# Spreading the preparation of the last weight matrix over the branch stage of a hybrid attention and retention step

## Chip, cores and metric

The kernel runs on one NeuronCore of a Trainium2 chip. The metric is the device time of one execution in microseconds (us); lower is better.

## What is computed

One layer of a streaming encoder on 2048 prompt frames and 64 sample frames of width 1024, all in fp32. The part that matters here is the end of the layer:

```python
def layer_output(x, oa, ob, za, zb, ga, gb, subln_g, lam_init, w_oa, w_ob, w_out):
    oa = (rmsnorm(oa, subln_g) * (1.0 - lam_init)).reshape(B, T, W_A) * jax.nn.silu(za)
    ob = rmsnorm(ob).reshape(B, T, W_B) * jax.nn.silu(zb)
    m = ga * (oa @ w_oa) + gb * (ob @ w_ob)      # the branch stage
    return x + m @ w_out                         # the last stage
```

`oa` and `ob` are the outputs of differential attention and of retention (512 columns each), `za`, `zb`, `ga`, `gb` come from a combined input projection, and `w_out` is 1024x1024.

## The kernel before

Each fp32 product is three matmuls on operands split in a high part (a cast to fp32r) and a low part (the fp32 value less its high part): high by high, high by low, low by high. A cast on ACT and a subtraction on DVE or POOL make the two parts.

The program is written by generators ("tasks") that a small loop advances by a cost model of its own. That loop fixes the order of the instructions on PE, ACT, DVE and POOL. The order of the DMAs, which all go through SyncE's queue (SP), is set afterwards by the framework's scheduler; SP then runs them strictly in that order, each waiting for what it needs. On every engine an instruction that waits holds up all that stand behind it.

Until 1576 us the projections, attention and retention run (matmul line L554 last). Then come:

- The **branch stage** (1576 to 1772 us). The 2112 frames are eight token groups of 264 columns. A group has eight tiles `ct` (128 rows of m each); a tile is 12 matmuls into PSUM bank `mm` (branch a) and 12 into bank `s` (branch b), two buffers each (L1722 to L1724). DVE multiplies each bank by its gate (L1742), which frees the bank; POOL adds the two (L1746); SP stores the sum to `mT` in DRAM. Groups and tiles are counted from 0 here, stores `mT` from 1 to 64.
- Its operands: `z` and `on` (132 KB each) are loaded, ACT takes silu of `z` (L1664), POOL multiplies (L1667), ACT casts to `ogh` (L1677), DVE subtracts to `ogl` (L1680). Four of these make the operands of one branch of one group (a "quad"). There is room for three quads: two in the tag `og`, one in the tag `ob`. A quad's casts wait until PE has finished with the quad three before it. Gates `gt` are loaded in pairs for one tile (10 buffers) and pass through ACT (L1698).
- The **preparation of w_out** (`b_prep`): w_out is used in blocks of Strassen's form. For each of four slices `c` it loads four pieces of 256 KB (`wst<-in_w_out_dram`), forms sums on DVE (L1758, four a slice) and splits seven blocks on ACT (L1815) and DVE (L1818). Slices 0 and 1 are split fully; of slices 2 and 3 the four sums t1 to t4 are held and split late (`b_late`) after tile 3 of group 7, when the buffers of w_o are free.
- The **last stage** (1772 us to the end): for each group seven products P1, P2, P6, P5, P7, P3, P4 of 12 matmuls (L1934) in banks `mm`, `s`, `at`. Their left operands are sums of quarters of m, loaded back from `mT` (`a<-mT`): s1, s2 on DVE (L1758), s3, s4 on POOL (L1756), split by L1853 and L1860. `y_prep` loads the quarters a11 and a12 of group 0; `y_load` loads all four quarters of each group for the sums. ACT copies the finished bank out as `u` (L1962), POOL adds the residual x (`oxt`), DVE finishes (L1984).

The buffers of the last stage (`u`, `oxt`, `ah`, `al`) and of w_out lie where earlier stages had theirs: the w_out blocks and `ob` over the buffers of the projections (among them `ev`, from which the last gates are stored by `gbT<-ev`), and `u`, `oxt`, `ah`, `al` over the gates of the branch stage.

Of the kernel before, what the change touches and what calls it, by code (L numbers as in the profile page):

```python
# [59 lines left out]
class Hybrid:  # L60
# [1573 lines left out]
    def out_prep(self):  # L1634
        pa = self.z3p
        self.wo = [[([[self.sb(self.zq, [128, 512], "wa", "woq", F32R) for n in "hl"],
                      [pa.tile([128, 512], F32R, tag=f"wo{n}{br}{kt}", name=f"wo{n}{br}{kt}") for n in "hl"]], {})
                    for kt in range(4)] for br in range(2)]
        for br in range(2):
            yield from self.load_wo(br, 0)  # L1640
        for g in range(8):
            gsl = slice(GW * g, GW * g + GW)
            for br, (oT, zT) in enumerate(((self.oaT, self.zaT), (self.obT, self.zbT))):
                for kt in range(4):
                    yield from self.take("oz", 2)
                    on = self.sb(pa, [128, GW], "oz", "on")
                    z = self.sb(pa, [128, GW], "oz", "z")
                    self.ld(z, zT[kt][:, gsl], 1 << 17)
                    t = self.ld(on, oT[kt][:, gsl], 1 << 17)
                    og = []  # L1650
                    self.ogs.append(og)
                    self.spawn(self.og_fin(on, z, t, og, (2 * g + br) % 3 == 2), 1)
                    yield self.pe
            if g == 0:
                self.spawn(self.gates(), 0)
                for q in range(1, 4):
                    for br in range(2):
                        yield from self.load_wo(br, q)
                yield lambda: self.b_left < 13

    def og_fin(self, on, z, t, og, third):
        nc = self.nc
# [98 lines left out]
    def b_raw(self, c, pool, tag):  # L1761
        w = self.i["w_out"][0]
        raw = {}
        for k, r, n in (("11", c, 0), ("12", c, 512), ("22", c + 4, 512), ("21", c + 4, 0)):
            yield from self.take(tag)
            raw[k] = self.sb(pool, [128, 512], tag, "wst")
            t = self.ld(raw[k], w[128 * r:128 * r + 128, n:n + 512], 1 << 18)
            self.b_left -= 1
        yield t + 600
        return raw  # L1770

    def b_prep(self):
        late = []
        for c in range(4):
            raw = yield from self.b_raw(c, self.z4, "st")
            for k in ("t1", "t2"):
                yield from self.take("st")
                raw[k] = self.sb(self.z4, [128, 512], "st", "wst")
            t1 = self.add(False, ALU.subtract, raw["t1"], raw["12"], raw["11"], self.pe)
            for k in ("11", "21", "22"):  # L1780
                t = yield from self.b_split(k, c, raw[k], self.pe)
            t3 = self.add(False, ALU.subtract, raw["12"], raw["22"], raw["12"], t)
            self.give("st", t3)
            yield t3
            t2 = self.add(False, ALU.add, raw["t2"], raw["12"], raw["11"], t3)
            self.give("st", t2)
            yield t2
            t4 = self.add(False, ALU.subtract, raw["21"], raw["21"], raw["t2"], t2)
            parts = [("t2", c, raw["t2"], t4), ("t1", c, raw["t1"], t1), ("t3", c, raw["12"], t3),
                     ("t4", c, raw["21"], t4)]  # L1790
            if c < 2:
                yield from self.b_fin(parts)
            else:
                late.append(parts)
        self.spawn(self.b_late([p for pair in zip(*late) for p in pair]), 1)
        self.spawn(self.y_prep(), 1)
# [24 lines left out]
        return t  # L1821

    def y_load(self):
        yield lambda: len(self.wt["t4"]) == 4
        for g in range(8):
            yield lambda: self.y_at >= g - 1 and len(self.mt[g]) == 8
            yield max(self.mt[g])
            raw = {}
            for k in ("a11", "a21", "a22", "a12"):
                raw[k], t = yield from self.y_raw(g, k)  # L1830
            self.yr.append((raw, t + 600))
# [223 lines left out]

    def out_stream(self):
        for g in range(8):
            og = []
            for ct in range(8):
                yield from self.m_tile(g, ct, og)  # L2060
        self.spawn(self.y_open(), 0)
        yield from self.y_group()
# [112 lines left out]
    def run(self):  # L2175
        tc, nc = self.tc, self.nc
        es = self.es = ExitStack()
        self.scratch()
        self.cp = es.enter_context(tc.tile_pool(name="cp", bufs=1))
        self.pp = es.enter_context(tc.tile_pool(name="pp", bufs=2, space=PSUM))  # L2180
        self.sp = es.enter_context(tc.tile_pool(name="small", bufs=6))
        z1 = self.z1 = ExitStack()
        z2 = self.z2 = ExitStack()
        self.ap = z1.enter_context(tc.tile_pool(name="att", bufs=ROWS, side="right"))
        self.tp_ = z1.enter_context(tc.tile_pool(name="tmp", bufs=1, side="right"))
        self.ep = z2.enter_context(tc.tile_pool(name="evac", bufs=2))
        self.wp = z2.enter_context(tc.tile_pool(name="wts", bufs=2))
        self.xp = z2.enter_context(tc.tile_pool(name="xT", bufs=1))
        nc.scalar.preload_act_table_set("natural_log_exp_and_others")
        self.marks = {}  # L2190
        self.gts, self.ya = {}, {}
        self.mt = [[] for _ in range(8)]
        self.wt = {k: [] for k in BLOCKS}
        self.b_left = 16
        for k in ("ac", "u", "xt", "ob"):
            self.res[k].free = []
        self.q_end = self.smx = None
        self.y_at, self.yr = -1, []
        self.yq = [{} for _ in range(8)]
        ET = mybir.EngineType  # L2200
        with tc.manual_schedule(engines=MANUAL(ET)):
            self.ident = self.cp.tile([128, 128], F32, tag="ident", name="ident")
            self.xraw = {(half, seg): [] for half in range(2) for seg in range(2)}
            self.xin = self.xsq = self.xfree = self.wloads = 0
            self.xacc = []
            self.xst, self.opened, self.rsb_of = None, False, None
            self.xr = [[None] * KC for _ in range(2)]
            self.rst, self.spread_ok, self.tb = [[], []], False, [None] * 9
            self.rs = self.cp.tile([128, 2, 10], F32, tag="rs", name="rs")
            self.ep_ = self.cp.tile([128, 2, 10], F32, tag="ep", name="ep")  # L2210
            self.gx = self.cp.tile([128, 8], F32, tag="gx", name="gx")
            self.ld(self.gx, self.i["norm_g"][0].rearrange("(c p) -> p c", p=128))
            self.ones_r = self.cp.tile([128, 128], F32R, tag="ones", name="ones")
            self.ones = self.ones_r.bitcast(F32)
            nc.vector.memset(self.ones, 1.0 / 128.0)
            self.epst = self.cp.tile([128, 1], F32, tag="epst", name="epst")
            nc.vector.memset(self.epst, EPS)
            self.warm(15)
            self.pe = 0.0
            self.spawn(self.consts(), 0)  # L2220
            self.spawn(self.w_stream(), 9)
            self.spawn(self.z_stream(), 4)
            self.loop()
        es.close()


def MANUAL(ET):
    return {ET.PE, ET.Activation, ET.DVE, ET.Pool}
# [65 lines left out]
```

## Time and profile before

| | us |
|---|---|
| Three runs: lowest, median, highest | 1944.82, 1947.86, 1949.27 |
| The profiled execution | 1945.97 |
| Its span in the trace | 1944.2 |
| Branch stage in the trace | 1576.1 to 1772.3 |
| Last stage in the trace | 1772.3 to 1944.2 |

The mean granted clock of TensorE is 0.999. Rows of an engine's timeline show the start, the duration, the line, the instruction and its tiles; in brackets stands how long the engine was idle before it and what ended that. The row count `x8` merges neighbours. PE's durations overlap: a 128x264 matmul lasts about 0.28 us, and one starts every 0.12 us. Rows of SPq are the issues of DMAs, not the transfers.

### The profile page before, as it was taken

The numbers are of one execution on the slowest core, as the hardware profiler recorded it, in microseconds if no ns is written. First come the engines' busy times: TensorE is split into PE (matmuls) and PEld (weight loads), VectorE is DVE, ScalarE is ACT, GpSimd is POOL, SyncE is SP. The second block draws the span as 40 slices with busy tenths as digits, with TensorE's granted clock in tenths as the row PEclk, the third lists the DMA queues.
The fourth block names the chain that finished last, engine by engine and source line by source line (L and its number), as shares of the span: only waits on it lengthen the run. The fifth ranks groups of instructions, "written<-read, shape, count | busy, mean of one in ns | idle before, by whom it ended". The sixth has DMA issues, their size and how long they took to land.

```text
span 1944.2 us, 33842 instructions
## 1 busy us (share of the span) xinstructions
PE 1927.8 (99%) x11984; PEld 1729.5 (89%) x11984; DVE 1163.8 (60%) x2798; ACT 967.3 (50%) x2072; POOL 488.8 (25%) x429
## 2 busy tenths in 40 slices
PE   9999999999999999999999999999999999999999
PEld 8779999999988899999998888888888889998887
DVE  6753777646666336648856757745764366545643
ACT  6443766544434235535765646544563455653321
POOL 4310112212121121211121112112112356543422
PEclk9999999999999999999999999999999999999999
DMA  7757554335566655664344253363233678866652
GB/s 230 242 154 196 143 147 129 107 104 155 164 193 186 163 151 164 202 187 142 112 116 131 72 146 101 95 182 118 68 98 103 187 233 265 265 191 195 191 147 66
DMA packets 372074, 303.32 MB, mean 156 GB/s; under 512 B 77440, under 2 KB 334720, under 8 KB 371904
## 3 DMA queue, kind: packets, MB, share of 16 engines
q1 hardware_dynamic: 371904, 301.16, 52.9%
q8 instruction: 94, 1.54, 0.3%
q14 instruction: 76, 0.62, 0.1%
HBM read 195.87 MB, written 100.14 MB: 152 GB/s over the span
## 4 chain that ended last, share of the span: by engine, by line
PE 89%; DVE 4%; DMA 2%; ACT 1%; issue 1%; POOL 1%; SPq 1%; DVEq 0%; ACTq 0%; POOLq 0%
PE mm L554 51%; PE mm L1934 4%; PE s L1052 3%; PE s L1053 3%; PE at L1160 3%; PE at L1934 2%; PE pv L1140 2%; PE pv L1139 2%; PE pv L1138 2%; PE mm L1722 1%; PE s L1723 1%; PE mm L1723 1%; PE mm L1724 1%; PE s L1724 1%; PE s L1934 1%
## 5 line engine op out<-in xcount | busy, mean ns | idle before, releaser
L514 POOL TENSOR_TENSOR wl<-ws,wh 128x512 fp32r<-128x512 f32 x191 | 261.4, 1379 | 897.0 <-ACT wh L504 552.7
L554 PE MATMUL mm<-xh,wh 128*128 128x512 f32 (+2 forms) x1280 | 460.7, 360 | 0.0
L554 PE MATMUL mm<-xh,wl 128*128 128x512 f32 (+2 forms) x1280 | 453.2, 354 | 0.0
L554 PE MATMUL mm<-xl,wh 128*128 128x512 f32 (+2 forms) x1280 | 451.5, 353 | 0.0
L554 PEld LDWEIGHTS mm<-xh,wl 128*128 128x128 f32 x1280 | 240.9, 188 | 32.1
L554 PEld LDWEIGHTS mm<-xh,wh 128*128 128x128 f32 x1280 | 241.2, 188 | 29.1 <-issue 0.2
L554 PEld LDWEIGHTS mm<-xl,wh 128*128 128x128 f32 x1280 | 241.5, 189 | 28.4
L554 PE MATMUL mm<-wh,xh 128*128 128x256 f32 (+1 forms) x768 | 236.8, 308 | 0.0
L554 PE MATMUL mm<-wh,xl 128*128 128x256 f32 (+1 forms) x768 | 231.3, 301 | 0.0
L554 PE MATMUL mm<-wl,xh 128*128 128x256 f32 (+1 forms) x768 | 231.3, 301 | 0.0
L1175 DVE TENSOR_TENSOR atl<-at,ath 128x512 fp32r<-128x512 f32 (+1 forms) x144 | 93.7, 659 | 136.2 <-ACT ath L1173 136.0
L504 ACT CAST wh<-ws 128x512 fp32r<-128x512 f32 x192 | 116.9, 617 | 112.3 <-PE mm L554 91.6
L1091 ACT ACTIVATE row<-row,a_mx 128x1024 f32<-128x1024 f32 (+7 forms) x160 | 153.7, 962 | 24.7 <-DVE a_mx L1071 24.6
L554 PEld LDWEIGHTS mm<-wh,xh 128*128 128x128 f32 x768 | 146.4, 191 | 7.2 <-issue 0.5
L554 PEld LDWEIGHTS mm<-wl,xh 128*128 128x128 f32 x768 | 146.5, 191 | 6.8 <-issue 0.5
L554 PEld LDWEIGHTS mm<-wh,xl 128*128 128x128 f32 x768 | 146.3, 191 | 5.6
L865 DVE TENSOR_TENSOR ev<-mm,rsb 128x512 f32<-128x512 f32 x140 | 83.0, 593 | 112.2 <-PE mm L554 110.4
L1173 ACT CAST ath<-at 128x512 fp32r<-128x512 f32 (+1 forms) x144 | 78.7, 563 | 141.9 <-PE at L1160 138.9
L1061 DVE CUSTOM_DVE_ANT_0 row<-s,dfar 128x512 f32<-128x512 f32 (+2 forms) x192 | 118.3, 630 | 46.3 <-PE s L1053 45.9
L1052 PE MATMUL s<-K,q 128*128 128x512 f32 (+3 forms) x320 | 118.3, 374 | 0.7 <-DVE a_acc L1061 0.7
L1053 PE MATMUL s<-K,q 128*128 128x512 f32 (+3 forms) x320 | 115.4, 363 | 0.0
L1110 ACT ACTIVATE row<-row,a_w 128x1024 f32<-128x1024 f32 (+4 forms) x96 | 85.1, 898 | 34.4 <-DVE a_w L1105 31.2
(342 smaller groups left out, 4188.1 us busy)
## 6 DMA issues: line engine op xcount, KB each, us to landing
ws<-in_w_in_dram SPq DMA_DIRECT2D x192, 256.0 KB, 3.1
q<-qT SPq DMA_DIRECT2D x128, 128.0 KB, 3.1
V<-vN SPq DMA_DIRECT2D x24, 512.0 KB, 5.5
K<-kT SPq DMA_DIRECT2D x48, 256.0 KB, 4.2
a<-mT SPq DMA_DIRECT2D x34, 256.0 KB, 4.2
gt<-gaT SPq DMA_DIRECT2D x64, 132.0 KB, 3.1
gt<-gbT SPq DMA_DIRECT2D x64, 132.0 KB, 3.0
mT<-gt SPq DMA_DIRECT2D x64, 132.0 KB, 3.1
```

Source lines behind the costliest of these rows:

```text
L504: self.nc.scalar.copy(h, st)
L514: self.nc.gpsimd.tensor_sub(l, st, h.bitcast(F32))
L554: nc.tensor.matmul(ps, p, q, start=c == 0 and i == 0, stop=c == KC - 1 and i == 2)
L865: nc.vector.tensor_mul(ev, ps, rsb)
L1052: nc.tensor.matmul(ps, q1s, kk, start=True, stop=False)
L1053: nc.tensor.matmul(ps, q2s, kk, start=False, stop=True)
L1061: nc.vector.tensor_tensor_reduce(out=units[k0 // 1024][:, k0 % 1024:k0 % 1024 + n], in0=ps, in1=tab, scale=-SLOPES[h], scalar=3.0e38, op0= ...
L1091: nc.scalar.activation(u, u, AF.Exp, bias=mx, scale=-1.0, accum_out=lp[:, k:k + 1])
L1110: nc.scalar.activation(u1, u1, AF.Identity, scale=w[:, 1:2])
L1173: nc.scalar.copy(ah[:, :w], at[:, :w])
L1175: nc.vector.tensor_sub(al[:, :w], at[:, :w], ah[:, :w].bitcast(F32))
L1934: nc.tensor.matmul(q[b], u, v, start=fresh and c == 0 and m == 0, stop=c == 3 and m == 2, skip_group_check=True)
```

## The change

`b_prep` now starts slice c at the beginning of token group 1, 3, 5 and 6 (`self.mg` is the group whose matmuls are being written out), where it ran through all four slices as fast as buffers allowed. `out_prep` no longer holds back the operands of group 1 until the first four pieces of w_out have been requested. `y_load` starts when three t1 blocks are split, where it waited for the fourth t4 block.

```diff
 def out_prep(self):
             if g == 0:
                 self.spawn(self.gates(), 0)
                 for q in range(1, 4):
                     for br in range(2):
                         yield from self.load_wo(br, q)
-                yield lambda: self.b_left < 13
 def b_raw(self, c, pool, tag):
             t = self.ld(raw[k], w[128 * r:128 * r + 128, n:n + 512], 1 << 18)
-            self.b_left -= 1
 def b_prep(self):
         late = []
-        for c in range(4):
+        for c, g in enumerate((1, 3, 5, 6)):
+            yield lambda: self.mg >= g
             raw = yield from self.b_raw(c, self.z4, "st")
 def y_load(self):
-        yield lambda: len(self.wt["t4"]) == 4
+        yield lambda: len(self.wt["t1"]) > 2
 def out_stream(self):
         for g in range(8):
-            og = []
+            og, self.mg = [], g
```

PE's order is the same, instruction for instruction; the other engines' orders are the same up to the start of the branch stage. Line numbers behind L1659 are one lower in the changed kernel.

**Start of the branch stage, DVE, before.** `gt<-gt,mm` and `gt<-gt,s` are the gate products of tiles 0, 1, 2; `wst` and `bl` belong to slice 0 of w_out; `ogl` is the low part of the first operand of group 1.

```order
L865 TENSOR_TENSOR ev_18280<-mm_18253,rsb_8967 128x512
L1742 SCALAR_TENSOR_TENSOR gt_17950<-gt_17950,mm_18331 128x264
L1742 SCALAR_TENSOR_TENSOR gt_17951<-gt_17951,s_18344 128x264
L1742 SCALAR_TENSOR_TENSOR gt_17954<-gt_17954,mm_18357 128x264
L1742 SCALAR_TENSOR_TENSOR gt_17955<-gt_17955,s_18373 128x264
L1758 TENSOR_TENSOR wst_18401<-wst_18305,wst_18303 128x512
L1818 TENSOR_TENSOR bl11_18290<-wst_18303,bh11_18289 128x512
L1742 SCALAR_TENSOR_TENSOR gt_17958<-gt_17958,mm_18387 128x264
L1742 SCALAR_TENSOR_TENSOR gt_17959<-gt_17959,s_18408 128x264
L1818 TENSOR_TENSOR bl21_18292<-wst_18309,bh21_18291 128x512
L1680 TENSOR_TENSOR ogl_18414<-on_18311,ogh_18413 128x264
```

The same place in the changed kernel:

```order
L865 TENSOR_TENSOR ev_18311<-mm_18269,rsb_8967 128x512
L1679 TENSOR_TENSOR ogl_18342<-on_18233,ogh_18341 128x264
L1679 TENSOR_TENSOR ogl_18346<-on_18237,ogh_18345 128x264
L1679 TENSOR_TENSOR ogl_18349<-on_18249,ogh_18348 128x264
L1679 TENSOR_TENSOR ogl_18352<-on_18253,ogh_18351 128x264
L1741 SCALAR_TENSOR_TENSOR gt_17950<-gt_17950,mm_18354 128x264
L1741 SCALAR_TENSOR_TENSOR gt_17951<-gt_17951,s_18379 128x264
L1741 SCALAR_TENSOR_TENSOR gt_17954<-gt_17954,mm_18398 128x264
L1741 SCALAR_TENSOR_TENSOR gt_17955<-gt_17955,s_18420 128x264
L1741 SCALAR_TENSOR_TENSOR gt_17958<-gt_17958,mm_18437 128x264
```

The four subtractions of group 1's first quad moved ahead of the first gate product, and the work on w_out left this place (it begins behind the gate product of tile 9).

**The same place in SP's queue, before:** the last store of the gates (`gbT<-ev`) and what follows it.

```order
L140 DMA gbT<-ev 128x2x256
L135 DMA wst<-in_w_out_dram 128x512 x4
L140 DMA mT<-gt 128x264 x2
L135 DMA gt<-gaT 128x264
L135 DMA gt<-gbT 128x264
L135 DMA on<-obT 128x264
L135 DMA z<-zbT 128x264
```

And in the changed kernel:

```order
L140 DMA gbT<-ev 128x2x256
L135 DMA wst<-in_w_out_dram 128x512 x2
L135 DMA z<-zaT 128x264
L135 DMA on<-oaT 128x264
L135 DMA z<-zaT 128x264
L135 DMA on<-oaT 128x264
L135 DMA z<-zaT 128x264
L135 DMA on<-oaT 128x264
L140 DMA mT<-gt 128x264
```

Six loads for group 2 stand ahead of the first store of a sum; five loads of group 1's branch b (`z<-zbT`, `on<-obT`), which followed the w_out pieces, now stand ahead of the `gbT` store. From the first w_out piece up to the gate load of tile 16, SP issues 71 DMAs before and 64 now; from there to the gate load of tile 24, 47 before and 44 now. Before, w_out pieces 9 to 16 stood between the stores `mT` 15 and 22; now pieces 5 to 8 stand between `mT` 12 and 15, pieces 9 to 12 between 28 and 31, and 13 to 16 between 44 and 47.

**Start of the last stage, POOL, before** (the last two additions of gates, the residual of P1, then s4 and s3):

```order
L1746 TENSOR_TENSOR gt_21107<-gt_21107,gt_21108 128x264
L1746 TENSOR_TENSOR gt_21154<-gt_21154,gt_21155 128x264
L1756 TENSOR_TENSOR u_21322<-u_21322,oxt_21299 128x512
L1756 TENSOR_TENSOR a_21341<-a_21249,a_21333 128x512
L1756 TENSOR_TENSOR a_21245<-a_21243,a_21245 128x512
```

And in the changed kernel:

```order
L1745 TENSOR_TENSOR gt_21107<-gt_21107,gt_21108 128x264
L1755 TENSOR_TENSOR a_21281<-a_21174,a_21259 128x512
L1755 TENSOR_TENSOR a_21150<-a_21144,a_21150 128x512
L1745 TENSOR_TENSOR gt_21164<-gt_21164,gt_21165 128x264
L1755 TENSOR_TENSOR u_21327<-u_21327,oxt_21329 128x512
```

s4 and s3 moved ahead of the last addition of gates. On SP, likewise, the four loads of group 1's quarters moved ahead of the last store `mT`; before:

```order
L135 DMA a<-mT 128x4x128 x3
L140 DMA mT<-gt 128x264 x4
L135 DMA oxt<-in_x_prompt_dram 128x512 x10
L135 DMA a<-mT 128x4x128 x4
L135 DMA oxt<-in_x_prompt_dram 128x512
```

now:

```order
L135 DMA a<-mT 128x4x128 x3
L140 DMA mT<-gt 128x264 x3
L135 DMA a<-mT 128x4x128 x4
L140 DMA mT<-gt 128x264
L135 DMA oxt<-in_x_prompt_dram 128x512 x12
```

The three `a<-mT` ahead of it are the rest of group 0's quarters, at the same place in both.

More of the change, by code (lines that the diff above doesn't have):

```diff
@@ L2193, in run @@
         self.wt = {k: [] for k in BLOCKS}
-        self.b_left = 16
+        self.mg = -1
         for k in ("ac", "u", "xt", "ob"):
```

## Prediction

> **What bounds the kernel now.** I read the busy times of the page first, then the stretches of the two stages that the change touches, then the timelines of PE, ACT, DVE and SP at each place where PE was idle. The page says that PE is the bound:
>
> ```profile
> span 1944.2 us, 33842 instructions
> PE 1927.8 (99%) x11984; PEld 1729.5 (89%) x11984; DVE 1163.8 (60%) x2798; ACT 967.3 (50%) x2072; POOL 488.8 (25%) x429
> ```
>
> PE's order and work don't change, so only PE's stalls, and a reduced clock behind them, can be won or lost. The stretches of the branch stage and of the last stage (length, then busy time and instructions of PE, weight loads, DVE, ACT, POOL, then granted clock, DMA share, GB/s) tell how much that is:
>
> ```profile
> 1576.10:1600.00 23.90, 23.11 (x187) 22.70 (x186) 18.62 (x29) 12.41 (x31) 15.61 (x17) 1.00 0.66 203
> 1600.00:1624.00 24.00, 23.82 (x196) 23.60 (x195) 19.23 (x34) 14.93 (x35) 16.38 (x17) 1.00 0.87 267
> 1624.00:1648.00 24.00, 22.85 (x186) 22.44 (x186) 16.68 (x33) 14.32 (x35) 14.14 (x17) 1.00 0.88 260
> 1648.00:1672.00 24.00, 21.26 (x157) 20.42 (x156) 14.44 (x31) 14.13 (x34) 14.46 (x16) 0.93 0.88 264
> 1672.00:1700.00 28.00, 28.00 (x232) 28.00 (x231) 12.92 (x30) 18.28 (x44) 14.56 (x19) 1.00 0.91 266
> 1700.00:1716.00 16.00, 15.94 (x131) 15.73 (x131) 8.53 (x19) 8.23 (x21) 8.67 (x12) 1.00 0.77 221
> 1772.30:1794.40 22.10, 20.17 (x87) 15.81 (x86) 9.69 (x14) 5.50 (x10) 8.03 (x6) 1.00 0.76 243
> 1805.56:1825.13 19.57, 19.57 (x85) 15.76 (x85) 12.92 (x18) 6.85 (x12) 9.62 (x7) 1.00 0.66 199
> ```
>
> The fifth row has no stall: 28.00 / 232 = 0.1207 us a matmul. At that pace the first four stretches lose 23.90 - 187 x 0.1207 = 1.3, then 0.3, 1.55 and 5.05 us, the sixth 0.2: 8.4 us in the branch stage. In the last stage an undisturbed group of products takes 19.57 us with 85 rows (0.23 each); the first has 22.10 with 87, so it loses 22.10 - 19.57 - 2 x 0.23 = 2.1 us. Together 10.5 us: the most that this change can win.
>
> Where PE lost them:
>
> ```profile
> 1591.63 0.39 PE L1722 MATMUL mm<-ogh,woh 128*128 128x264 f32 x1 [0.79 <-DVE gt L1742]
> 1626.58 0.39 PE L1722 MATMUL s<-ogh,woq 128*128 128x264 f32 x1 [0.39 <-ACT ogh L1677]
> 1653.19 0.39 PE L1722 MATMUL s<-ogh,woq 128*128 128x264 f32 x1 [2.00 <-ACT ogh L1677]
> 1656.18 0.42 PE L1722 MATMUL s<-ogh,woq 128*128 128x264 f32 x1
> 1656.40 0.42 PE L1723 MATMUL s<-ogl,woq 128*128 128x264 f32 x1
> 1782.40 0.50 PE L1934 MATMUL at<-bht,al 128*128 128x512 f32 x1 [1.20 <-DVE al L1860]
> 1785.72 0.50 PE L1934 MATMUL mm<-bht,ah 128*128 128x512 f32 x1 [0.73 <-ACT u L1962]
> ```
>
> In group 0 a bank came free late; at the starts of groups 2 and 3 the quad of branch b was cast late; and behind the 2.00 us wait the matmuls start 0.22 instead of 0.12 us apart (the clock of 0.93 in the fourth stretch). Why were the casts late? ACT's queue:
>
> ```profile
> 1582.41 0.62 ACT L1815 CAST bh<-wst 128x512 fp32r<-128x512 f32 x1 [12.61 <-DMA wst<-in_w_out_dram]
> 1624.77 0.93 ACT L1698 ACTIVATE gt<-gt,bg 128x264 f32<-128x264 f32 x2 [0.84 <-DMA gt<-gaT]
> 1652.32 0.51 ACT L1698 ACTIVATE gt<-gt,bg 128x264 f32<-128x264 f32 x1 [1.02 <-DMA gt<-gbT]
> 1652.74 0.39 ACT L1677 CAST ogh<-on 128x264 fp32r<-128x264 f32 x1
> ```
>
> Both times the casts stood behind gates (tiles 16 and 24) that still waited for their loads. And at the start ACT stood 12.61 us at the first w_out piece with group 1's silu behind it. The loads come late because SP and the DMA rings are full, 260 to 267 GB/s in the three stretches:
>
> ```profile
> 1577.04 0.37 SPq L140 DMA_DIRECT2D gbT<-ev  x1
> 1579.36 0.33 SPq L135 DMA_DIRECT2D wst<-in_w_out_dram  x1
> 1604.37 2.51 SPq L135 DMA_DIRECT2D wst<-in_w_out_dram  x4
> 1620.31 0.42 SPq L135 DMA_DIRECT2D gt<-gaT  x1
> 1647.53 0.38 SPq L135 DMA_DIRECT2D gt<-gaT  x1
> ```
>
> The last two are the gate loads of tiles 16 and 24, 71 and 47 issues on: 0.577 and 0.579 us an issue.
>
> **The change, part by part.** The sum is made against the profiled execution, 1945.97 us (its span plus 1.8), 1.9 below the median of the runs; the difference is then taken from the median.
>
> *The held-back operands and slice 0 leaving group 0.* ACT no longer meets a w_out piece at 1569, so group 1's silu and products run there under the last projection. What becomes late instead: group 1's first quad now stands on DVE ahead of the first gate product. Its parts go to `ob` buffers that lie over `ev`, so they may have to wait for the last `gbT` store, as the w_out piece did, and that store has five more loads ahead of it on SP:
>
> ```profile
> 1577.04 2.19 DMA gbT<-ev
> 1581.93 0.28 PE L1722 MATMUL mm<-ogh,woq 128*128 128x264 f32 x1
> 1600.47 2.24 DVE L1680 TENSOR_TENSOR ogl<-on,ogh 128x264 fp32r<-128x264 f32 x3
> 1654.20 3.04 DVE L1680 TENSOR_TENSOR ogl<-on,ogh 128x264 fp32r<-128x264 f32 x7
> ```
>
> The store lands at 1579.2, a cast takes 0.4, four subtractions 1.7 (by 3.04 / 7) to 3.0 (by 2.24 / 3), the gate product 0.4: tile 2's bank is free at 1581.7 to 1583.0 where PE wants it at 1581.93. With up to 1 us more for the store, the cost is 0 to 2.1 us; I take 0.5, nearer the fast row, since POOL has less to do there. The 0.8 us stall at 1591 goes, because the five w_out operations between the gate products go. Group 0 loses 0.5 instead of 1.3; I leave the 0.3 of the next stretch.
>
> *Groups 2 and 3.* The gate load of tile 16 is now 64 issues behind the first w_out piece: 1579.4 + 0.5 + 64 x 0.577 = 1616.8, 3.5 us earlier. PE gets there 0.8 us earlier and had waited 1.55, so 3.5 - 0.8 - 1.55 leaves 1.1 to spare: no stall. Tile 24's load comes at 1616.8 + 44 x 0.579 = 1642.3, 5.2 us earlier. PE gets there 0.8 + 1.55 = 2.35 earlier and its waits of the fourth stretch were 5.05 less some 1.4 of slow clock (24 us x 0.07 is 1.7, part of it while PE stood), 3.65. 5.2 - 2.35 - 3.65 = -0.8: a stall of 0.8 stays, too short for the slow clock, which the trace shows only behind the 2.00 us one (not behind 1.20). Bounds: nothing, or 1.6 and 2.5 if the issues cost more than 0.58 us with a fuller queue.
>
> *Slices 1 to 3 in groups 3, 5 and 6, slice 0 in group 1.* The same operations at the same prices:
>
> ```profile
> L1758 DVE TENSOR_TENSOR wst<-wst 128x512 f32<-128x512 f32 x16 | 15.3, 958 | 3.0 <-DMA wst<-in_w_out_dram 2.9
> L1818 DVE TENSOR_TENSOR bl<-wst,bh 128x512 fp32r<-128x512 f32 x12 | 10.6, 886 | 3.5 <-ACT bh L1815 3.5
> ```
>
> Now at most three of them stand between two tiles' gate products, under 3 us; a bank has two buffers, so PE comes back to it 4.35 us (three half tiles of 12 x 0.1207) after it filled it. They are covered; if a piece lands late, they hold the gate products and PE stops. I take 0.3 for slice 0 (counted) and 0.2 each for 1 to 3; bounds 0 and the 1.3 us of the first stretch for each. The branch stage then loses 0.5 + 0.3 + 0.8 + 0.6 + the sixth row's 0.2 = 2.4: it wins 6.0 us.
>
> *The earlier sums of group 0.* These rows show the start of the last stage:
>
> ```profile
> 1765.92 8.58 SPq L140 DMA_DIRECT2D mT<-gt  x4
> 1772.85 1.85 DVE L1758 TENSOR_TENSOR a<-a 128x512 f32<-128x512 f32 x2
> 1773.07 1.09 POOL L1746 TENSOR_TENSOR gt<-gt 128x264 f32<-128x264 f32 x1 [2.19 <-DMA mT<-gt]
> 1774.18 1.71 DMA mT<-gt
> 1776.07 0.59 ACT L1962 COPY u<-mm 128x512 f32<-128x512 f32 x1 [9.49 <-DMA mT<-gt]
> 1780.52 2.97 POOL L1756 TENSOR_TENSOR a<-a 128x512 f32<-128x512 f32 x2
> ```
>
> The last store `mT` landed at 1775.9 and only then could ACT write `u`. The quarters were there in time and keep their place on SP; s1 and s2 move from 1772.85 to about 1770, ahead of the last gate products, and s4 and s3 from 1780.5 to about 1771.3. So the two waits (1.20 on s1's low part, 0.73 on the copy behind s3's cast) lose their cause. But POOL's last addition now stands behind s4 and s3 (2.97 us by the row): from 1773.07 to about 1774.2. With it the store, `u`, and the casts of s2 move by 1.1 us, and by some 0.5 more because loads now stand ahead of the store. P6 of group 0 started at 1777.5 without a wait on them; it will wait about 1.6 plus a little for s2's low part: 1.8 us. Bounds: 0.5 (if POOL's two sums overlap the wait for the gate product) and 4. I win 2.1 - 1.8 = 0.3.
>
> Sum: 6.0 + 0.3 = 6.3 us. 1945.97 - 6.3 = 1939.7; from the median, 1947.86 - 6.3 = 1941.6.
>
> **The rivals.**
>
> *A. The queue stays the bound.* The bytes are the same, and SP asks for pieces 5 to 8 in groups 1 and 2, not 3. If an issue costs 0.65 instead of 0.577 us there, tile 16's load is at 1621.5 and tile 24's at 1650: no gain at either. For it: 260 GB/s or more in three stretches. Against it: the fifth runs at 266 GB/s without a stall. Then the 0.8 of group 0 and about 1 us of slow clock are the gain: 1946.0.
>
> *B. The last store waits for the loads ahead of it.* The store alone took 1.71 us; the loads of three quarters:
>
> ```profile
> DMA to landing us min/median/max: 3.3/3.7/4.1
> ```
>
> If the store, issued at 1775.3, lands only with the fourth load (1774.5 + 4.1, and 0.5 for its own bytes) at 1779.1, P6 waits 3.2 us and the clock may drop as at 1653 (1.4): the last stage loses 4.6, the sum is 3.5, the time 1944.4. The Trainium skill's page "DMA: Bandwidth & Descriptors" (Queues, rings and completion order) says that each DMA engine consumes descriptors in ring order and a completion is written after the engine's earlier writes, which would bring this about; no row of the trace has such a store right behind such loads.
>
> *C. Slower: the first store holds the queue.* SP meets the first `mT` store before group 2's fourth pair, and POOL makes that sum behind group 1's products, which wait for `ob`, for the `gbT` store. Before, SP had it out by here:
>
> ```profile
> 1583.84 0.38 SPq L135 DMA_DIRECT2D gt<-gaT  x1
> ```
>
> I expect the gate load of tile 5, this row, at about 1586; its gate is wanted when bank `mm` of tile 5 is full, at 1576.1 + 5.5 tiles of 2.9 = 1592.1, and the load takes about 4, like those quoted under B. Later than 1588, every such microsecond stops PE and moves all loads. At 1594, 6 us are lost there and stay lost, since slices 0 and 1 leave SP no slack to catch up, and groups 2 and 3 wait as before: 1947.86 + 6 - 2 = 1952. Against it: the products' loads are nearly all out by 1573.
>
> **How the numbers follow.** A change within 0.2% (3.9 us) can't be told from none here. My forecast has 0.6, and 0.9 of that lies below 1943.9 (its own range 1937.4, when all 10.5 us go, to 1944.5, with 2.5 in group 3 and 2.1 in group 0); A 0.18; B 0.12, half below the mark; C 0.1, four fifths above 1951.8. Faster 0.54 + 0.06 + 0.05 for A coming out mild = 0.65; slower 0.08; the rest, 0.27, the same. The range goes from 1937 to 1947, which leaves out C and the tails.
>
> **What would show it.** Right: no PE wait for `ogh` above 1 us in groups 2 and 3, no clock below 1.00 in the fourth stretch, and about 2.4 us lost in the whole branch stage. The gate product of tile 0 later than 1580, behind four `ogl` rows, shows the first term; the last `mT` store landing at 1777.5 and a PE wait at P6, not P5, the last. Wrong: waits for `ogh` that only move (A), a wait above 3 us at P6 (B), a PE wait for gates in group 0 (C).

## The result and the profile after

The changed kernel takes 1956.36 us (median of six runs, 1953.22 to 1957.45) against 1947.93 for the kernel before in the same session: a ratio of 1.0040, 95% interval 1.0030 to 1.0051. It is 8 us slower, clear of the noise. The forecast was 1941.6, and its range ended at 1947. The profiled execution took 1956.91 us:

```profile
span 1955.1 us, 33894 instructions
PE 1935.0 (99%) x11984; PEld 1734.9 (89%) x11984; DVE 1160.1 (59%) x2798; ACT 966.8 (49%) x2072; POOL 487.0 (25%) x429
```

PE ran the same 11984 matmuls. What differs is where it stood. The stretches of the branch stage after the change, in the columns of the prediction:

```profile
1576.10:1600.00 23.90, 23.90 (x199) 23.90 (x198) 9.34 (x25) 10.97 (x30) 12.27 (x17) 1.00 0.74 225
1600.00:1624.00 24.00, 23.92 (x197) 23.72 (x195) 18.57 (x34) 14.87 (x35) 15.13 (x16) 1.00 0.75 225
1624.00:1648.00 24.00, 23.71 (x191) 23.29 (x191) 7.95 (x21) 11.14 (x28) 10.54 (x15) 1.00 0.77 231
1648.00:1672.00 24.00, 22.02 (x151) 21.17 (x152) 16.94 (x31) 15.48 (x38) 13.89 (x15) 0.86 0.76 221
1700.00:1716.00 16.00, 13.71 (x95) 12.82 (x95) 9.94 (x20) 9.96 (x26) 7.93 (x10) 0.89 0.71 201
1740.00:1764.00 24.00, 20.78 (x145) 20.21 (x144) 12.60 (x25) 11.35 (x25) 5.91 (x8) 0.86 0.55 154
```

The last of these stretches in the kernel before was full:

```profile
1740.00:1764.00 24.00, 24.00 (x199) 24.00 (x198) 10.97 (x24) 13.82 (x30) 6.47 (x8) 1.00 0.55 155
```

The first three stretches are better than before (199 matmuls in the first, where it had 187). The fourth is a little worse (151 for 157), and in two later ones, which had lost nothing or almost nothing, 36 (95 for 131) and 54 matmuls (145 for 199) are missing, at a clock of 0.89 and 0.86. The DMA share fell from 0.87 and 0.88 to 0.75 and 0.77: the queue is no longer full, and yet loads come late.

PE's waits between 1560 and 1955 us, in total, times and the longest, and below them the matmuls that waited long, with the next three behind one of them:

```profile
PE s L1721 <- ACT ogh L1676: 7.0, 3, 3.2
PE mm L1933 <- ACT ah L1852: 1.8, 1, 1.8
```
```profile
1649.98 0.56 PE L1721 MATMUL s<-ogh,woq 128*128 128x264 f32 x1 [2.07 <-ACT ogh L1676]
...
1703.65 0.39 PE L1721 MATMUL s<-ogh,woq 128*128 128x264 f32 x1 [1.72 <-ACT ogh L1676]
...
1756.67 0.59 PE L1721 MATMUL s<-ogh,woq 128*128 128x264 f32 x1 [3.22 <-ACT ogh L1676]
...
1757.52 0.42 PE L1723 MATMUL s<-ogh,woq 128*128 128x264 f32 x1
1757.74 0.42 PE L1721 MATMUL s<-ogh,woq 128*128 128x264 f32 x1
1757.96 0.42 PE L1722 MATMUL s<-ogl,woq 128*128 128x264 f32 x1
...
1789.24 0.47 PE L1933 MATMUL mm<-bht,ah 128*128 128x512 f32 x1 [1.82 <-ACT ah L1852]
```

Three times, at the starts of groups 3, 5 and 7, the first matmul of branch b waits for casts on ACT, and behind it, until 1656.9, 1708.1 and 1762.7 us, the matmuls start 0.22 us apart or more. To compare kernels I add up, over PE's timeline, by how much the distance between two starts exceeds 0.1207 us (0.233 for the 512 columns of the last stage). Neighbouring starts that are late together count as one place, and only places over 0.3 us are counted:

| us lost in | groups 0-2 | group 3 | groups 4-6 | group 7 | last stage | sum | span |
|---|---|---|---|---|---|---|---|
| before | 3.4 | 5.2 | 0.3 | 0 | 2.5 | 11.4 | 1944.2 |
| after | 0.8 | 6.0 | 6.0 | 6.5 | 3.9 | 23.2 | 1955.1 |

The sums differ by 11.8, the spans by 10.9. So these places hold the loss. ACT's timeline shows what the casts stood behind:

```profile
1649.11 0.52 ACT L1697 ACTIVATE gt<-gt,bg 128x264 f32<-128x264 f32 x1 [0.49 <-DMA gt<-gbT]
1649.53 1.33 ACT L1676 CAST ogh<-on 128x264 fp32r<-128x264 f32 x4
...
1702.47 0.51 ACT L1697 ACTIVATE gt<-gt,bg 128x264 f32<-128x264 f32 x1 [1.04 <-DMA gt<-gbT]
...
1703.20 2.59 ACT L1676 CAST ogh<-on 128x264 fp32r<-128x264 f32 x8
...
1754.87 0.62 ACT L1852 CAST ah<-a 128x512 fp32r<-128x512 f32 x1 [3.59 <-DMA a<-mT]
...
1756.22 1.34 ACT L1676 CAST ogh<-on 128x264 fp32r<-128x264 f32 x4
```

In groups 3 and 5 the casts stand behind a gate whose load has just landed; in group 7 behind two gates and, ahead of them, the cast of the first quarter of group 0's sums, for whose load ACT stood idle 3.59 us. SP's waits between 1580 and 1716 us for a store's landing, before and then after:

```profile
SPq L135 <- DMA mT<-gt: 1.6, 1, 1.6
```
```profile
SPq L135 <- DMA mT<-gt: 22.7, 22, 2.5
```

A gate load takes the buffer that the store of the fifth tile before it still reads; SP now comes to that load before the store has landed, and all later loads stand behind it. All waits of SP that the profile names in this window, these included, came to 27 us before and 40 us after.

### The profile page after: what moved, and what is told of

The parts are those of the page before. It is cut to its first block, busy times and chain, and to the rows that moved or that the text cites. A ratio compares the mean times of both kernels' runs of the same rounds, so it can differ in the third digit from the quotient of the medians.

```text
span 1955.1 us, 33894 instructions
## 1 busy us (share of the span) xinstructions
PE 1935.0 (99%) x11984; PEld 1734.9 (89%) x11984; DVE 1160.1 (59%) x2798; ACT 966.8 (49%) x2072; POOL 487.0 (25%) x429
```

## The experiments

All were timed beside the kernel before, and each ratio is to it. The losses come from one profiled execution of each. Where a kernel has more lines, the three matmuls are L1724 to L1726 (not L1721 to L1723), the gate L1700, its product L1744, the low part of a quad L1679.

**1. The hold alone.** The hold is the line that keeps group 1's operands back until four pieces of w_out have been requested.

```diff
-                yield lambda: self.b_left < 13
```

> The kernel before with one line taken out: the loads of the branch outputs no longer wait until four pieces of the last matrix are under way. The matrix is still prepared as in the kernel before, and the first token group's sums are loaded as late as there. Blocked-queue theory (SP stands on gate loads that wait for the landing of the store which frees their buffer, and the order that does it comes from taking out the hold): SP's waits of a load on a store of gate products between 1580 and 1716 us rise from 1.6 us to over 10 us, groups 3 to 5 lose some 8 to 12 us on TensorE, time 1951 to 1956. Rival (the pieces of the matrix in the middle groups do the harm): those waits stay under 6 us, time 1945 to 1950.

1946.22 us, ratio 0.9993 (0.9984 to 1.0001): the rival's number. The losses are the same as before in kind: 3.0 us in groups 0 to 2, 5.4 in group 3, 0.6 in groups 4 to 6, none in group 7, 2.4 in the last stage. SP waited 4.9 us for stores. In groups 5 to 7 the casts wait for PE alone, not behind a gate:

```profile
1700.48 0.73 ACT L1676 CAST ogh<-on 128x264 fp32r<-128x264 f32 x2 [0.60 <-PE mm L1722]
```

Taking out the hold does no harm.

**2. Hold taken out and pieces spread, the sums of group 0 as before.**

```diff
-                yield lambda: self.b_left < 13
-        for c in range(4):
+        for c, g in enumerate((1, 3, 5, 6)):
+            yield lambda: self.mg >= g
```

> The whole change but the earlier loads of the first token group's sums. If those loads cost nothing, as the trace of the changed kernel lets one think (group 7's 6.5 us hang on the first quarter's cast, which this edit doesn't move, and P6 in the last stage on where the last store stands), the time is that of the changed kernel less 0 to 2 us: 1954 to 1957, with group 7's loss of about 6.5 us still there. Rival (the earlier loads carry the loss): within 0.2% of the kernel before, 1945 to 1951.

1954.32 us, 1.0029 (1.0017 to 1.0040): in the range of the theory, though group 7 lost 4.2 us and not the 6.5 that it named. Groups 3 and 4 to 6 lose 6.2 and 5.9 us, SP waits 22.1 us for stores. The last stage loses 2.4 as before.

**3. More gate buffers in the changed kernel.** The lines that give the new buffers back are not shown.

```diff
+GE = set(range(11, 64, 6))
-        "oz": 11, "og": 16, "ob": 8, "gt": 10, "wa": 16, "st": 13, ...
+        "oz": 11, "og": 16, "ob": 8, "gt": 10, "ge": 2, "wa": 16, "st": 12, ...
-            yield from self.take("gt", 2)
-            pair = [self.sb(self.z3p, [128, GW], "gt") for _ in range(2)]
+            tag, pool = ("ge", self.z4) if n in GE else ("gt", self.z3p)
+            yield from self.take(tag, 2)
+            pair = [self.sb(pool, [128, GW], tag) for _ in range(2)]
```

> The changed kernel with one more pair of buffers for gate tiles (every sixth gate from the 12th on takes it) and one staging buffer fewer for the last matrix. Blocked-queue theory: a gate load then waits for the store of the sixth tile before it and not of the fifth, so SP's waits of a load on a store between 1580 and 1716 us fall from 22.7 us to under 8 us, and the 12.3 us that groups 3, 4 and 5 lose fall to under 5 us: time 1945 to 1950 if group 7 still loses its 6.5 us or less. Rival (the pieces of the matrix, not the buffers, make the casts late): groups 3 to 5 still lose over 9 us, time 1954 to 1959.

1955.20 us, 1.0032 (1.0020 to 1.0045). My theory missed. The lead of the gate loads grew (tile 16's was issued 6.7 us ahead of the tile's first matmul, not 3.3), but the loop that orders the work also put more gates ahead of the casts, and SP went on waiting:

```profile
SPq L136 <- DMA mT<-gt: 17.9, 18, 2.1
```

Groups 3, 4 to 6 and 7 lost 3.6, 8.7 and 1.8 us. So two more buffers alone don't mend it; as the order on ACT changed with them, this does not show what they would do without that.

**4. The first quarter behind group 7.**

```diff
             if g == 0:
+                yield lambda: len(self.ogs) > 63 and self.ogs[63]
                 for k in ("a11", "a12"):
```

> The changed kernel, with the first quarter (a11) of the first token group's sums loaded and cast only behind the casts of the last group's branch outputs. Theory (in group 7 TensorE waits for casts that stand on ACT behind the cast of that quarter, whose load SP issues late): group 7's loss of about 6.5 us falls under 1.5 us, the groups ahead are as before, the last stage may lose up to 2 us more since the quarter comes later: time 1949 to 1953. Rival (the group 7 casts would come as late without it, since SP's queue is behind): over 4 us of that loss stay, time 1954 to 1958.

1951.81 us, 1.0020 (1.0011 to 1.0028), in the range of the theory: group 7 lost 1.1 us instead of 6.5, groups 3 to 6 nearly as much as ever (10.7 for 12.0). The last stage gave 1.9 us of it back, 5.8 for 3.9, at its third product, P6:

```profile
1784.01 0.77 PE L1934 MATMUL mm<-bht,ah 128*128 128x512 f32 x1 [2.81 <-DMA a<-mT]
```

So that cast is what group 7 waited for, but a later place for it has its own price. (The profile puts P6's wait down to the load. By ACT's timeline it ended with the cast of s2 at 1783.9, behind the copy `u`, which waited for the last store `mT`. The gate products ahead of that store had stood on DVE behind a sum that waited 2.32 us for a quarter.)

**5. Casts ahead of the gates in the changed kernel.** The theory was now that the order on ACT decides, not the queue.

```diff
     def gate(self, n, ct, pair, t):
+        if n > 8 and ct >= 0:
+            k = n - ct + 7
+            yield lambda: len(self.ogs) > k and self.ogs[k]
         yield t
```

> The changed kernel with one rule more: the gates of a group go to ScalarE only behind the casts of that group's second quad. The third run has weakened the theory of too few gate buffers: gate loads were issued some 3 us sooner there and SP's waits on stores fell only from 22.7 to 17.9 us, yet groups 3 and 5 still lost 3.6 and 4.2 us, behind casts that stood on ScalarE behind gates still being loaded. Theory now (the order on ScalarE: a slice makes the gate loads late, and the casts, which have all they need, stand behind them): the 10.7 us of groups 3 and 5 fall to under 3 us, group 7 keeps up to 6.5 us for the first quarter's cast, time 1946 to 1950. Rival (the queue as a whole is behind by what each slice takes, so TensorE then waits for the gates' products, over a PSUM buffer, instead): the loss returns as waits for the products of L1741's kind and the time is 1953 to 1957.

1947.54 us, 1.0001 (0.9993 to 1.0010): with this rule the whole change costs nothing. No group but the last waits more than 0.3 us for casts any more:

```profile
PE mm L1724 <- DVE gt L1744: 5.2, 5, 1.7
PE s L1724 <- ACT ogh L1676: 2.2, 2, 1.9
```

Group 3 loses nothing, groups 4 to 6 7.7 us (most of it in waits for gate products, where the rival is right), group 7 2.8 (behind the first quarter's cast again), the last stage 0.7: 11.2 in all for 23.2. The gate loads are no earlier for it. Their lead, worked out from the timelines as the start of a tile's first matmul less SP's issue of its `gbT` load:

| lead in us at tile | 24 | 36 | 42 | 48 | 54 |
|---|---|---|---|---|---|
| before | 1.6 | 5.3 | 8.1 | 5.4 | 2.6 |
| after | -0.3 | 0.3 | 4.9 | 3.2 | -0.3 |
| 1, hold alone | -0.9 | 5.6 | 7.2 | 6.3 | 5.5 |
| 5, casts first | 1.8 | -2.4 | -0.5 | 0.8 | 0.1 |

In the changed kernel the lead falls to zero, a stall of PE gives it back (tile 42 stands behind the stall of group 5), and it falls again. In the fifth run it stays near zero and little is lost, since a gate is wanted only when a bank has to come free, the casts at once. The rule moved rows on DVE and SP too, as the loop ordered the work anew (the low parts also come ahead of the gate products), so the order on ACT and that on DVE aren't told apart.

**6. The same rule without the spread.** Experiment 1 and the rule of experiment 5 together.

> The kernel before without the hold (the first experiment) and with the same rule: a group's second casts ahead of its gates on ScalarE. Nothing is spread. By the order theory the 5.4 us that group 3 lost in the first experiment fall to under 1.5 us and the rest stays: 1941 to 1944, under both kernels. By the rival (the queue is behind as a whole) group 3 loses the same in waits for gate products: 1945 to 1949.

1942.11 us, 0.9974 (0.9964 to 0.9984): under both kernels, but the expected number came from the wrong place, which is luck. Group 3 still lost 5.5 us, and the last stage, which had lost 2.4, lost nothing. In group 3 the casts now stand behind a silu whose load is late, a gate and a piece of w_out:

```profile
1649.59 0.42 ACT L1663 ACTIVATE z<-z 128x264 f32<-128x264 f32 x1 [3.18 <-DMA z<-zbT]
1650.26 0.93 ACT L1700 ACTIVATE gt<-gt,bg 128x264 f32<-128x264 f32 x2 [0.24 <-DMA gt<-gaT]
1651.10 0.60 ACT L1817 CAST bh<-wst 128x512 fp32r<-128x512 f32 x1
1651.61 1.34 ACT L1676 CAST ogh<-on 128x264 fp32r<-128x264 f32 x4
```

**7. The earlier sums alone.**

```diff
-        yield lambda: len(self.wt["t4"]) == 4
+        yield lambda: len(self.wt["t1"]) > 2
```

> The kernel before with only the condition for loading the first token group's sums changed. Four of those loads then stand on SP ahead of the last store. If that costs, as the changed kernel's last stage lets one think (3.9 us lost there against 2.5): 1948.5 to 1950.5. If not: within 1 us of the kernel before.

1948.21 us, 1.0002 (0.9993 to 1.0011): no cost to be told from none. The profiled execution shows the last stage losing 3.7 us, as in the changed kernel, with a wait of 1.9 us for `ah` at P6; group 3's stall had moved to group 2 there.

**8. The spread alone.** The hold needs the first four pieces early, so slice 0 stays in group 0.

```diff
-        for c in range(4):
+        for c, g in enumerate((0, 3, 5, 6)):
+            yield lambda: self.mg >= g
```

> The kernel before with the pieces of the last matrix spread over groups 0, 3, 5 and 6, and the hold kept (it needs the first slice in group 0). If each slice eats some 5 us of the gate loads' lead and a stall at the next group's start gives it back, the harm is the spread's and does not need the hold to be gone: groups 4 to 7 lose over 8 us, time 1951 to 1956. Rival (only spread and hold together do harm): within 0.2% of the kernel before, 1945 to 1951.

1954.16 us, 1.0031 (1.0019 to 1.0043): the theory's number. Group 3 loses only 0.6, groups 4 to 6 9.9, group 7 3.2:

```profile
1702.15 0.39 PE L1722 MATMUL s<-ogh,woq 128*128 128x264 f32 x1 [2.05 <-ACT ogh L1677]
...
1729.39 0.39 PE L1722 MATMUL s<-ogh,woq 128*128 128x264 f32 x1 [1.34 <-ACT ogh L1677]
...
1762.39 0.39 PE L1722 MATMUL mm<-ogh,woq 128*128 128x264 f32 x1 [2.94 <-DVE gt L1742]
```

The spread carries the loss, with or without the hold.

**9. Both mends in the changed kernel** (experiments 4 and 5 together).

> The changed kernel with both mends: a group's second casts ahead of its gates, and the first quarter (a11) behind the casts of group 7. In the fifth run 2.8 us were left in group 7 and 5.2 us in waits for gate products. If group 7's are the first quarter's, they go: 1943 to 1946, with 0 to 3 us of it given back in the last stage, where the fourth run waited 2.8 us for that quarter. If they are the queue's, the time stays that of the fifth run, 1946.5 to 1949.

1955.00 us, 1.0032 (1.0019 to 1.0044): missed. Group 7 lost 4.1 us in waits for gate products, and the last stage 7.1, most of it here:

```profile
1787.36 0.47 PE L1937 MATMUL mm<-bht,ah 128*128 128x512 f32 x1 [3.63 <-ACT ah L1855]
```

The rows ahead of this cast say why. It stood behind ACT's copy `u`, which could start only at 1786.16, when the last store `mT` had landed. POOL's addition for that store came only behind s4 and s3, 2.4 us after the last gate product, and the store itself, issued behind four loads of quarters, took 3.35 us to land. So the later quarter cost the last stage more than the 2.8 us that it had cost group 7. Why group 7 now waits for gate products isn't shown.

**10. The pieces of w_out issued by ACT, casts first.**

```diff
-            t = self.ld(raw[k], w[128 * r:128 * r + 128, n:n + 512], 1 << 18)
+            self.nc.scalar.dma_start(raw[k], w[128 * r:128 * r + 128, n:n + 512])
+            self.dma = max(self.dma, self.pe) + (1 << 18) / 300.0
+            t = self.dma + DMA_LAT
-            yield lambda: self.mg >= g
+            yield lambda: len(self.ogs) > 8 * g + 7 and self.ogs[8 * g + 7]
```

> The fifth run's kernel (changed kernel, casts first) with the pieces of the last matrix issued by ScalarE instead of SP, each slice behind its group's casts. The bytes are the same, SP has 16 loads fewer to issue. If what a slice takes from the gate loads is their place in SP's queue, the lead of the gate loads stays above 2 us and the 5.2 us of waits for gate products fall under 2 us: 1943 to 1946. If it is the bytes (16 pieces of 256 KB at some 230 GB/s are 18 us of transfer), the waits stay over 4 us and the time is 1946.5 to 1951 with what ScalarE now spends on issuing.

1958.79 us, 1.0058 (1.0045 to 1.0071): outside both. It doesn't tell the two apart, since ACT itself stood at the issues with silu and gates behind it, and PE then waited 6.82 us for a gate product (until 1661.35):

```profile
1651.25 6.50 ACTq L1769 DMA_DIRECT2D wst<-in_w_out_dram  x4
1657.80 0.42 ACT L1663 ACTIVATE z<-z 128x264 f32<-128x264 f32 x1 [8.14 <-DMA on<-obT]
```

**11. The sixth run's kernel, each slice begun behind a group's casts.**

```diff
         for c in range(4):
+            yield lambda: len(self.ogs) > 8 * c + 7 and self.ogs[8 * c + 7]
             raw = yield from self.b_raw(c, self.z4, "st")
```

> The sixth run's kernel (no hold, casts first) with each slice of the last matrix begun only behind a group's second casts: groups 0, 1, 2 and 3. The sixth run still lost 5.5 us in group 3, where those casts and their low parts stood behind pieces of the matrix on ScalarE and VectorE and behind a z load. If that order is the cause, group 3 loses under 1.5 us: 1937 to 1940. If the queue is behind whatever stands first, 4 us or more are lost in groups 2 to 4: 1941 to 1945.

1940.80 us, 0.9963 (0.9949 to 0.9976), the lowest median of the study and 0.8 us above the expected range. In the profiled execution, the slowest of its five with 1943.66 us, group 3 lost 1.5 us, as the order theory had it, all groups together 6.7, the last stage nothing:

```profile
PE s L1725 <- DVE ogl L1679: 2.5, 5, 1.1
PE mm L1724 <- DVE gt L1744: 1.3, 2, 0.8
```

Its interval and that of experiment 6 overlap, so the two are not told apart.

## Why the prediction was wrong

- *PE's order and work don't change, so only stalls can be won or lost.* Right: in the two kernels and the eleven others the span less the losses, counted as in the table, is 1932 to 1935 us.
- *10.5 us are the most that can be won.* No kernel here won more, and the fault lay in stopping there. I costed what the first four stretches would win back and treated the rest of the stage, which lost nothing, as safe. The bounds of the sum had no term for new stalls in groups 4 to 7 but 0 to 1.3 us a slice; they lost 12.5 us together. (One bound is also added up wrong: with 2.5 us in group 3 and 2.1 in group 0 the terms give 1944.9, not 1944.5.)
- *The held-back operands, group 0: 0.5 us lost instead of 1.3.* Right. The casts waited for the last `gbT` store as described, tile 0's gate product came at 1580.42 behind four `ogl`, and the first stretch shows no loss. With the low loss of the two stretches behind it, this gave 2.6 us (0.8 lost for 3.4).
- *Groups 2 and 3.* Half right. Group 2's stall went. Tile 16's load came at 1617.86, 1.1 us after the forecast 1616.8. Tile 24's came 44 issues later, as counted, but at 1645.09 instead of 1642.3, which is 0.619 us an issue and not 0.579; and its partner `gbT` another 1.44 us behind it, where I had 0.58. These rows show it:

```profile
1617.86 0.38 SPq L135 DMA_DIRECT2D gt<-gaT  x1
...
1645.09 0.32 SPq L135 DMA_DIRECT2D gt<-gaT  x1
1646.53 0.32 SPq L135 DMA_DIRECT2D gt<-gbT  x1
```

  and SP's waits for a store's landing between 1617.8 and 1646.6 us:

```profile
SPq L135 <- DMA mT<-gt: 5.5, 5, 2.0
```

  The price per issue was taken from stretches in which SP never waited for such a landing. In the new order SP comes to gate loads whose buffer is not free: of the 28.7 us between the first and the last of these rows 5.5 are such waits. A wait of 2.07 us stayed where I had 0.8, and the slow clock that I had ruled out by the length of the wait came with it: 6.0 us.
- *Slices 1 to 3 at 0.2 us each.* This is the step that failed. I asked whether a slice's work on DVE fits between two gate products, and it does. I did not ask what each slice takes from the lead of the gate loads, nor what stands behind a late gate on ACT, although the rows of groups 2 and 3 in the prediction show just that: casts behind gates that wait for loads. Spread over the stage, the lead falls to zero again after each of slices 1 to 3, and what brings it back is a stall (the table of experiment 5). In the kernel before, the same pieces took it early, in groups 0 to 3, and behind the stall of group 3 the lead did not fall to zero again.
- *The earlier sums of group 0: 0.3 us won.* P6's wait was forecast at 1.8 and came at 1.82, by luck. That POOL's last addition would end some 1.1 us later behind s4 and s3 was right (2.29 us after the last gate product, 1.23 before). But the store behind it took 3.12 us to land where it had taken 1.71, so 1.4 us and not 0.5 came from the loads ahead of it. That was offset because P6 had 0.5 us to spare (its first matmul started at 1777.8 before; 1777.5, as the prediction has it, is its weight load) and because it waited for the cast of s2, not for the low part. The rows are the issues of the four loads, the store's way from issue to landing, and the copy that waited for it:

```profile
1781.24 3.18 SPq L135 DMA_DIRECT2D a<-mT  x4
1784.78 3.12 DMA mT<-gt
1788.04 0.58 ACT L1961 COPY u<-mm 128x512 f32<-128x512 f32 x1 [13.13 <-DMA mT<-gt]
```

  The forecast had no slow clock behind this wait; it cost 1.9 us more. Alone the edit costs nothing that can be measured (experiment 7).
- *What I did not see at all:* with `b_prep` ending in group 6, `y_prep`'s first quarter moves from group 3 or 4 to group 7 on ACT, ahead of that group's casts. In the program `y_prep` starts where `b_prep` ends, so it moved with it. The place cost 3.2 us of wait and about as much slow clock.
- *The rivals.* A had the cause in kind, a queue that gives nothing back, but ended at no gain. B was right in its mechanism, though not in its size: the last store landed 0.4 us behind the fourth of the loads ahead of it. In the five kernels with three or four such loads directly ahead (the changed one and experiments 3, 7, 9 and 10) it took 3.1 to 3.4 us, in the other eight 1.7 to 1.8. C had SP standing at an `mT` store, at another place. None of them let the spread itself stall later groups, so none reached 1956.

What is shown: the spread carries the loss (experiments 2 and 8, against 1 and 7), and putting a group's casts and low parts ahead of its gates takes that loss away (5). Without the spread the rule alone left group 3's loss as it was (6); with each slice behind the casts as well most of it went (11). What stays open: what of a slice makes the gate loads late, its bytes, its issues or the waits for stores that come with a queue that is no longer full. SP's waits for a store's landing between 1580 and 1716 us do go with the spread: 15.7 to 22.7 us in the eight kernels that have it, 1.6 to 5.3 in the five without. But experiment 5 has 18.8 us of them and is no slower than the kernel before, so they alone do not make the loss. Experiments 3 and 10 were meant to tell the three apart and don't settle it. What the last stage lost, 0 to 7 us, changed from order to order. One part can be named: in the six kernels whose P6 waited for the cast of s2 (the changed one and experiments 3, 4, 7, 9 and 10) it started 1.2 us behind ACT's copy `u`, and `u` waited for the last store. The rest is not worked out.

## What to carry to other kernels

Spreading a burst of loads need not lower its cost. Here the burst took the lead of the other loads early and once, the spread took it again and again, and stalls paid it back. Look at what stands in line behind the work that becomes late, engine by engine, at every place where the spread touches the stage, also where nothing is lost today. Work that has all it needs and that the bound engine wants at once belongs ahead of work that waits for a load; that rule took some 8 us off the changed kernel (experiment 5), and with the hold gone and the slices behind the casts 7 us off the kernel before (experiment 11). A store that others wait for pays for the loads issued just ahead of it.

## What the hardware showed that was not expected

A wait's length does not tell what it costs. Behind 1.72 us (group 5 after) PE ran at half pace to 1708.1 us and the place cost 4.7 us. Behind 1.94 us in experiment 5 it ran at full pace at once, one matmul later:

```profile
1752.30 0.39 PE L1724 MATMUL s<-ogh,woq 128*128 128x264 f32 x1 [1.94 <-ACT ogh L1676]
1753.05 0.39 PE L1725 MATMUL s<-ogl,woq 128*128 128x264 f32 x1 [0.37 <-DVE ogl L1679]
1753.28 0.28 PE L1726 MATMUL s<-ogh,woq 128*128 128x264 f32 x1
1753.40 0.28 PE L1724 MATMUL s<-ogh,woq 128*128 128x264 f32 x1
```

Behind the 2.94 us of experiment 8 (at 1762.39) the place cost 3.2 in all, so there was no half pace either.

What decides can be read from the granted clock. In every trace the changes of the clock in the branch stage and behind it lie whole multiples of 3.413 us apart. In the changed kernel the clock is halved from 1650.04 to 1656.86, 1704.65 to 1708.06, 1755.85 to 1762.68 and 1789.98 to 1793.40 us. So I divided the traces into periods of that length and counted the matmuls that PE starts in each period of the branch stage that runs at full clock; 28 fit. All 16 periods with 10 or fewer were followed by a period at half clock, one of the four with 11 or 12, and none of the 705 with 13 or more. Three periods after the change (6 matmuls start in the first), then two of experiment 8 (15 start in each), in the columns of the prediction; the rows also count matmuls that began just before:

```profile
1701.24:1704.65 3.41, 1.21 (x8) 0.80 (x7) 1.02 (x2) 2.37 (x8) 0.75 (x1) 1.00 0.54 152
1704.65:1708.06 3.41, 3.32 (x13) 2.84 (x14) 3.41 (x10) 2.38 (x8) 0.87 (x1) 0.50 0.54 157
1708.06:1711.48 3.42, 3.42 (x30) 3.42 (x29) 1.56 (x6) 1.44 (x3) 0.75 (x1) 1.00 0.82 226
1757.45:1760.87 3.42, 2.01 (x17) 1.79 (x15) 0.00 (x0) 0.21 (x1) 0.00 (x0) 1.00 0.73 196
1760.87:1764.28 3.41, 1.89 (x15) 1.89 (x16) 2.09 (x6) 2.15 (x5) 1.45 (x2) 1.00 0.52 139
```

The wait of 1.72 us, with the gaps of the matmuls behind it, fell into one period. That of 2.94 us lay across the border of two, and so did the 1.94 us of experiment 5. Where this grid stands differs from trace to trace by up to a whole period, and no kernel here controls it.

The Trainium skill's page "TensorE: Matmul & The Clock Gate" (Part 1: The HAM clock gate) says that activity is judged in windows of some 3.4 us that run freely, and the traces agree, with 3.413 us. But it says that the slow state comes after an idle window of about 3.4 us, and here periods in which PE still started up to 10 of 28 matmuls were enough.
